# Hybrid decoder step: six pairs of gate tiles beside FoX in place of four, twelve single tiles beside the scans in place of sixteen

## The chip, the core and the metric

The kernel runs on one core of one Trainium2 chip. The metric is the device time of one execution in microseconds (us); less is better. Three runs of the kernel before gave 1921.46, 1922.18 and 1924.54 us, so its median is 1922.18 us.

## The reference

One layer of a hybrid decoder is computed for 1024 prompt tokens and 32 sample tokens, 1056 columns in all, with a model width of 1024. The tokens are normed, multiplied by one wide input projection, and the result feeds three token mixers: GLA (a gated linear scan), FoX (softmax attention with a forget bias) and HGRN2 (another gated scan). Each mixer's output goes through a branch matrix, is scaled by a sigmoid gate of its own, and the three are added:

```python
z = xn @ w_in      # gq gk gv glr gr | fq fk fv ff | hq hf hi hg | ga gb gc
merged = (sigmoid(ga) * (o_a @ w_branch_a) + sigmoid(gb) * (o_b @ w_branch_b)
          + sigmoid(gc) * (o_c @ w_branch_c))
x = x + merged @ w_out
x = x + (silu(h @ w_ffn_gate) * (h @ w_ffn_up)) @ w_ffn_down
```

What matters here are the 24 tiles of gates: ga, gb and gc have 1024 output rows each, which is 8 tiles of 128 rows each. A gate tile is nothing but a piece of the input projection; it is written to DRAM and read back when its branch tile is made.

## The kernel before

**Two ways to project a tile.** Every weight and activation is held as a high part and a low part, and a product is three TensorE matmuls (high by high, high by low, low by high). A single tile (`gemm`, L118) takes 3 column chunks of 352, 8 blocks of the inner dimension and 3 products: 72 matmuls of 352 columns, and three evictions by VectorE (L672, a multiply by the norm factor). A pair of tiles (`pair_run`, L1905) is made by a Strassen-like scheme with 7 products in place of 8: 7 products, 2 column quarters, 4 blocks, 3 products, that is 168 matmuls of 264 columns (L1941) for two tiles. Its weight sums, splits and evictions are VectorE and ScalarE work.

**Which tile goes which way.** `PAIRS` (L55 to L60) lists the tiles that go in pairs: 8 FoX tiles, 16 tiles for the scans, the gates GATES[24 - 2 * NGP:20] (at NGP = 4 these are gc 0 to 3), 12 tiles of gr, hq and hg, and gates gc 4 to 7. That is 44 tiles in 22 pairs. `TILES` (L61) are the rest: four FoX tiles, made early, and ga 0 to 7 and gb 0 to 7, made one by one.

**The stages around the change.**

1. `in_pairs` (L574) runs the 22 pairs. After each of a pair's 14 column quarters `beside` pumps one step of the FoX background work (`fox_head`, `fox_sample`), so a pair offers 14 steps. What is left at the end is drained (L637).
2. `phase_m` (L350) sets up the scans: two GLA pairs and four HGRN heads. They are generators in four queues: `bg3` and `bg4` (gates, decay, scan), `bgs` (the sample part of a scan) and `bgn` (`head_norm`, L1121). `bgn` runs one norm at a time, in order.
3. `mixer_jobs` (L676) projects the 16 single gate tiles. After each block of three matmuls `tick` (L195) pumps one step of one queue, in turn; when only one queue holds work, every second tick is skipped. So a tile offers 24 steps. The last tile is made by `gemm_tiles` (L151) and offers none.
4. `out_jobs` (L1577) makes 24 branch tiles, of 36 matmuls of 352 columns each, which offer 12 ticks each. The first eight are branch b (FoX), which doesn't need the scans. Before the last mixer tile, `first` (L1640) loads a gate and then asks for four free buffers for the FoX outputs; where they aren't free, it pumps steps with no matmuls between them:

```python
            while len(self.u.free) < 4:
                self.tick()
            ts.extend(fetch_o(order[0][0]))
```

5. After the sixth branch tile (AHEAD = 6, L1674) `ranges` (L1658) drains all four queues and then calls `any_range` (L1559), which reads a flag and branches (L1563): a recomputation of all scans that is skipped here. No instruction is laid across this branch, so all background work stands before it.

**A head norm** (`head_norm`, L1121) is: square on ScalarE (L1128), three matmuls of 352 columns with the ones matrix (L1135), three VectorE scalings (L1136), Ln and Exp on ScalarE (L1139, L1143), three VectorE steps of a Newton iteration (L1147, L1149, L1152), two VectorE multiplies (L1154, L1156), and a store (L1159).

**Order.** The program is laid out when the kernel is built: for each engine the instructions are put in an order in which those emitted earlier rank ahead of those emitted later, and one that isn't ready by the layout's own reckoning can be overtaken by a later one that is. On the chip each engine then keeps its order.

**After it** come the other 18 branch tiles, the output projection, the FFN in pairs, and the final norm. None of these is touched.

Of the kernel before, what the change touches and what calls it, by code (L numbers as in the profile page):

```python
# [50 lines left out]

FOX = [(n, h) for h in range(4) for n in ("fq", "fk", "fv")]
NFP = 4
NGP = 4
PAIRS = FOX[4:4 + 2 * NFP]  # L55
GATES = [(n, t) for n in ("ga", "gb", "gc") for t in range(8)]
PAIRS += [(n, t) for n, c in (("gq", 2), ("gk", 2), ("gv", 4), ("hf", 4), ("hi", 4)) for t in range(c)]
PAIRS += GATES[24 - 2 * NGP:20]
PAIRS += [(n, t) for n in ("gr", "hq", "hg") for t in range(4)]
# [2311 lines left out]
```

## Time and profile before

| what | us |
|---|---|
| median of three runs | 1922.18 |
| the profiled execution, its own time | 1923.73 |
| the profiled execution, span of the core | 1921.9 |
| last matmul of the pairs, first matmul of the single gate tiles | 651.08 |
| 11 of the 16 gate tiles done | about 871.6 |
| last matmul ahead of the branch at L1563 | about 1009.2 |
| first matmul behind it | 1015.05 |

The profiled execution's time is the span and 1.83 us around it, and it lies 1.55 us above the median. The page gives busy time of each engine over the span; the window view gives it for stretches, with the clock that was granted to TensorE as a share of full speed; the timeline gives instructions in the order of time, with the idle time of the engine before them and what released it.

### The profile page before, as it was taken

The numbers are of one execution on the slowest core, as the hardware profiler recorded it, in microseconds if no ns is written. First come the engines' busy times: TensorE is split into PE (matmuls) and PEld (weight loads), VectorE is DVE, ScalarE is ACT, GpSimd is POOL, SyncE is SP. The second block draws the span as 40 slices with busy tenths as digits, with TensorE's granted clock in tenths as the row PEclk, the third lists the DMA queues.
The fourth block names the chain that finished last, engine by engine and source line by source line (L and its number), as shares of the span: only waits on it lengthen the run. The fifth ranks groups of instructions, "written<-read, shape, count | busy, mean of one in ns | idle before, by whom it ended". The sixth has DMA issues, their size and how long they took to land. (4 is left out here: it accounts for less than half of the span.)

```text
span 1921.9 us, 36877 instructions
## 1 busy us (share of the span) xinstructions
PE 1894.2 (99%) x14846; PEld 1805.1 (94%) x14846; DVE 1322.9 (69%) x2395; ACT 836.9 (44%) x1470; POOL 44.0 (2%) x82
## 2 busy tenths in 40 slices
PE   9999999999999999999998999999999999999997
PEld 7999999999999988888898999999999999999997
DVE  7866656644666587687676755976666666568976
ACT  8444444322433355454554433634344333332435
POOL 0000000100000000000000000000000000000000
PEclk9999999999999999999998999999999999999999
DMA  4443332577666533343446443243331221423212
GB/s 170 163 146 116 115 127 83 170 238 243 205 210 186 186 115 138 125 147 131 140 159 235 147 146 116 86 153 127 120 104 68 78 99 55 182 93 117 87 61 91
DMA packets 99574, 263.33 MB, mean 137 GB/s; under 512 B 14850, under 2 KB 28354, under 8 KB 99394
## 3 DMA queue, kind: packets, MB, share of 16 engines
q1 hardware_dynamic: 97842, 259.69, 39.6%
q8 instruction: 118, 1.93, 0.4%
q10 hardware_dynamic: 1296, 0.67, 0.1%
q0 software_dynamic: 256, 0.52, 0.1%
q14 instruction: 62, 0.51, 0.1%
HBM read 188.60 MB, written 72.24 MB: 136 GB/s over the span
## 5 line engine op out<-in xcount | busy, mean ns | idle before, releaser
L139 PE MATMUL pg<-x,wh 128*128 128x352 f32 x1692 | 428.7, 334 | 6.7 <-DVE u L1622 6.0
L1941 PE MATMUL pg<-x,wh 128*128 128x264 f32 x2080 | 399.1, 287 | 0.9 <-DVE du L1950 0.5
L1941 PEld LDWEIGHTS pg<-x,wh 128*128 128x128 f32 x2080 | 322.8, 188 | 6.2 <-issue 2.6
L139 PEld LDWEIGHTS pg<-x,wh 128*128 128x128 f32 x1692 | 294.4, 189 | 28.3 <-issue 14.4
L1941 PE MATMUL pg<-x,wl 128*128 128x264 f32 x1040 | 295.5, 284 | 1.1 <-DVE wl L228 1.1
L139 PE MATMUL pg<-x,wl 128*128 128x352 f32 x846 | 275.1, 325 | 0.0
L1941 PEld LDWEIGHTS pg<-x,wl 128*128 128x128 f32 x1040 | 195.6, 188 | 1.6 <-DVE wl L228 1.6
L1941 PE MATMUL pg<-x,rh 128*128 128x264 f32 x976 | 186.2, 286 | 0.2 <-DVE fu L1950 0.2
L1941 PE MATMUL pg<-pr,wh 128*128 128x264 f32 x832 | 161.1, 291 | 0.0
L139 PEld LDWEIGHTS pg<-x,wl 128*128 128x128 f32 x846 | 160.4, 190 | 0.4 <-issue 0.3
L1941 PEld LDWEIGHTS pg<-x,rh 128*128 128x128 f32 x976 | 151.2, 188 | 2.0 <-issue 1.3
L227 ACT ACTIVATE wh<-wf 128x512 fp32r<-128x512 f32 (+2 forms) x125 | 77.5, 620 | 149.1 <-PE pg L1941 122.9
L1941 PE MATMUL pg<-x,rl 128*128 128x264 f32 x488 | 139.0, 285 | 0.0
L1941 PEld LDWEIGHTS pg<-pr,wh 128*128 128x128 f32 x832 | 129.0, 188 | 4.1 <-issue 2.6
L228 DVE TENSOR_TENSOR wl<-wf,wh 128x512 fp32r<-128x512 f32 (+2 forms) x125 | 84.9, 680 | 48.7 <-ACT wh L227 45.4
L1941 PE MATMUL pg<-pr,wl 128*128 128x264 f32 x416 | 118.3, 284 | 0.0
L110 ACT ACTIVATE wh<-wf 128x1024 fp32r<-128x1024 f32 (+2 forms) x60 | 51.4, 856 | 148.6 <-PE pg L139 125.3
L1950 DVE TENSOR_TENSOR pu<-pu,pg 128x264 f32<-128x264 f32 x132 | 56.1, 427 | 69.5 <-PE pg L1941 67.1
L1950 DVE TENSOR_TENSOR fu<-fu,pg 128x264 f32<-128x264 f32 x132 | 56.3, 429 | 66.7 <-PE pg L1941 66.5
L1952 ACT ACTIVATE fu<-pg 128x264 f32<-128x264 f32 x176 | 66.8, 384 | 62.7 <-PE pg L1941 62.7
L1952 ACT ACTIVATE pu<-pg 128x264 f32<-128x264 f32 x176 | 66.7, 382 | 62.6 <-PE pg L1941 62.2
L1941 PEld LDWEIGHTS pg<-x,rl 128*128 128x128 f32 x488 | 91.7, 188 | 0.1
(496 smaller groups left out, 3966.6 us busy)
## 6 DMA issues: line engine op xcount, KB each, us to landing
z_dram<-pu SPq DMA_DIRECT2D x44, 528.0 KB
wf<-in_wgu SPq DMA_DIRECT2D x44, 512.0 KB
u<-z_dram SPq DMA_DIRECT2D x38, 528.0 KB
wf<-in_winp SPq DMA_DIRECT2D x30, 512.0 KB
fa<-in_kc SPq DMA_DIRECT2D x48, 256.0 KB
fa<-in_vc SPq DMA_DIRECT2D x48, 256.0 KB
wf<-in_win SPq DMA_DIRECT2D x19, 512.0 KB
a_dram<-fu SPq DMA_DIRECT2D x18, 528.0 KB
```

Source lines behind the costliest of these rows:

```text
L110: nc.scalar.activation(wh[:, :n], wf[:, :n], AF.Copy)
L139: nc.tensor.matmul(ps[:m, :CW], a[:, k, :], b[:, sl], start=n == 0, stop=n == 3 * job.kt - 1)
L227: nc.scalar.activation(h, x, AF.Copy)
L228: nc.vector.tensor_tensor(l, x, h.bitcast(F32), ALU.subtract)
L1941: nc.tensor.matmul(ps, a[:, w], b, start=first and m == 0, stop=m == 3 * K - 1, skip_group_check=not first)
L1950: nc.vector.tensor_tensor(out, out, ps, ALU.add)
L1952: nc.scalar.activation(out, ps, AF.Copy)
```

## The change

One constant goes from 4 to 6. GATES[24 - 2 * NGP:20] grows from 4 tiles to 8, so gb 4 to 7 join the pairs (24 pairs in place of 22), placed just ahead of gc 0 to 3; `TILES` loses them, and 12 single gate tiles are left, with gb 3 the last of them in place of gb 7. AHEAD, the queues, the number of buffers and the order of the branch tiles stay.

```diff
 FOX = [(n, h) for h in range(4) for n in ("fq", "fk", "fv")]
 NFP = 4
-NGP = 4
+NGP = 6
 PAIRS = FOX[4:4 + 2 * NFP]
 GATES = [(n, t) for n in ("ga", "gb", "gc") for t in range(8)]
 PAIRS += [(n, t) for n, c in (("gq", 2), ("gk", 2), ("gv", 4), ("hf", 4), ("hi", 4)) for t in range(c)]
```

## Rows read from the trace of the kernel before

**Rows 1.** The page: span, and busy time of each engine.
```profile
span 1921.9 us, 36877 instructions
PE 1894.2 (99%) x14846; PEld 1805.1 (94%) x14846; DVE 1322.9 (69%) x2395; ACT 836.9 (44%) x1470; POOL 44.0 (2%) x82
```

**Rows 2.** Windows: stretch, length, busy of PE, PEld, DVE, ACT, POOL; granted clock; DMA.
```profile
676.00:871.60 195.60, 193.83 (x1417) 166.21 (x1415) 148.15 (x331) 103.03 (x170) 9.42 (x18) 1.00 0.35 123
871.60:895.70 24.10, 24.10 (x154) 20.80 (x155) 22.39 (x56) 13.00 (x28) 0.48 (x2) 1.00 0.36 125
871.60:1009.20 137.60, 136.75 (x871) 123.39 (x871) 98.56 (x183) 68.85 (x92) 0.48 (x2) 1.00 0.44 150
1009.20:1014.50 5.30, 0.00 (x0) 0.00 (x0) 0.72 (x2) 0.38 (x1) 0.00 (x0) 0.67 0.45 161
1015.00:1021.30 6.30, 6.25 (x21) 6.25 (x22) 1.38 (x3) 3.01 (x3) 0.00 (x0) 0.50 0.93 335
```

**Rows 3.** Windows, L139 alone (352 columns), then L1941 alone (264 columns).
```profile
1032.00:1196.00 164.00, 164.00 (x1015) 163.83 (x1014) 1.00 0.42 148
1232.00:1640.00 408.00, 408.00 (x3354) 408.00 (x3354) 1.00 0.28 99
```

**Rows 4.** Timeline of PE: last matmuls of FoX, first matmuls of the single gate tiles.
```profile
619.99 0.60 PE L1076 MATMUL pg<-f_ident,fa 128*128 128x128 f32 x4
...
651.08 0.49 PE L139 MATMUL pg<-x,wh 128*128 128x352 f32 x2
```

**Rows 5.** Timeline of DVE: eviction and weight split of a single tile.
```profile
871.06 0.53 DVE L672 TENSOR_TENSOR ub<-pg,r 128x352 f32<-128x352 f32 x1 [0.18 <-PE pg L139]
...
872.95 1.22 DVE L111 TENSOR_TENSOR wl<-wf,wh 128x1024 fp32r<-128x1024 f32 x1
```

**Rows 6.** Timelines of SP, DVE, PE: three instructions that show what is laid ahead.
```profile
889.56 0.33 SPq L1608 DMA_DIRECT2D u<-z_dram  x1
...
879.99 0.14 DVE L1548 TENSOR_REDUCE rg_m<-range 128x1 f32<-128x6 f32 x1
...
905.66 0.27 PE L1551 MATMUL pg<-c_ident,rg_m 128*1 128x128 f32 x1
```

**Rows 7.** Timeline of PE: matmuls of a head norm between those of a branch tile.
```profile
976.73 0.76 PE L1135 MATMUL pg<-ub,ones 128*128 128x352 f32 x2
977.06 0.76 PE L139 MATMUL pg<-x,wh 128*128 128x352 f32 x2
```

**Rows 8.** Timeline of DVE: the last head norm.
```profile
996.54 0.52 DVE L1136 TENSOR_SCALAR u<-pg 128x352 f32<-128x352 f32 x1
...
1001.13 1.26 DVE L1147 SCALAR_TENSOR_TENSOR u<-u,u 128x1056 f32<-128x1056 f32 x1 [0.60 <-ACT u L1143]
...
1002.74 1.25 DVE L1149 TENSOR_TENSOR u<-u,u 128x1056 f32<-128x1056 f32 x1
...
1004.34 1.25 DVE L1152 SCALAR_TENSOR_TENSOR u<-u,u 128x1056 f32<-128x1056 f32 x1
...
1006.10 1.31 DVE L1154 SCALAR_TENSOR_TENSOR ub<-ub,c_hng,u 128x1056 f32<-128x1056 f32 x1
1007.45 1.26 DVE L1156 TENSOR_TENSOR ub<-ub,u 128x1056 f32<-128x1056 f32 x1
```

**Rows 9.** Timeline of ACT: the same head norm, with a table load inside it.
```profile
997.09 1.09 ACT L1139 ACTIVATE u<-u 128x1056 f32<-128x1056 f32 x1 [4.66 <-DVE u L1136]
...
998.71 1.28 ACT L1143 ACT_TABLE_LOAD   x1
1000.01 1.09 ACT L1143 ACTIVATE u<-u 128x1056 f32<-128x1056 f32 x1
```

**Rows 10.** Timeline of SP: the store of the last head norm.
```profile
1008.74 0.33 SPq L1159 DMA_DIRECT2D o_dram<-ub  x1
```

**Rows 11.** Timeline of PE: either side of the branch at L1563.
```profile
1008.75 0.32 PE L139 MATMUL pg<-x,wl 128*128 128x352 f32 x1
1015.05 0.95 PE L139 MATMUL pg<-x,wh 128*128 128x352 f32 x2 [5.97 <-DVE u L1622]
```

## The prediction

> **What bounds the kernel now.** I began with the page: TensorE is busy for 1894.2 of 1921.9 us [rows 1], so a change pays by the TensorE time it removes, unless it uncovers something. Busy alone can hide waits, since matmuls are pipelined, so next I took the pace of gap-free stretches from the windows view: 164.00 us for 1015 matmuls of 352 columns is 0.1616 us each, 408.00 us for 3354 of 264 columns is 0.1216 us each [rows 3]. Then I read the stage that the change shortens, the scans. From 676 to 1009.2 us TensorE is never idle for long, and VectorE is busy for three quarters of the time [rows 2]. TensorE sets the time here, and the single tiles' matmuls are what covers the scans' waits. The timelines last: the last norm of the background work stores its result at 1008.74 us [rows 10], in the same microsecond in which the last matmul ahead of the branch starts [rows 11]. So background work and matmuls run out together at this point. That balance is what the change moves.
>
> **The matmuls.** Four single tiles go: 4 x 72 x 0.1616 = 46.5 us. Two pairs come: 2 x 168 x 0.1216 = 40.9 us. TensorE saves 5.7 us, if each stage stays covered. The added pairs need no FoX work beside them and give it no help: its last matmuls lie at 620 us, 31 us (one and a half pairs) ahead of the first single gate tile [rows 4], so the steps offered there find empty queues already. Weights and stores are as many bytes as before, only earlier on SP's queue. The gate tile gb 0 is stored three tiles ahead of its reload in place of seven, still over 30 us. The pairs' sums, splits and evictions stay under their matmuls, as in the FFN stretch, where TensorE is full [rows 3]. All this I cost at nothing.
>
> By a rule of the Trainium skill this part would come out otherwise. The page "TensorE: Matmul & The Clock Gate", section "Back-to-back issue gap", gives 81 ns per matmul at 128 columns and 131 ns at 512 for streams with weight loads; a straight line between them, an estimate, has 98.7 ns at 264 columns and 110.2 ns at 352, so two pairs would cost 33.2 us against 31.7 us for four tiles, and the sum below would end 7.1 us higher. The trace disagrees, with 121.6 and 161.6 ns, a ratio of 0.753 against 264/352 = 0.75 [rows 3]; I keep the measured pace.
>
> **What the four tiles covered.** The first eleven single tiles keep their place, so up to the point that was 871.6 us the scans go as before. Following the generators in the code from there, 136 background steps are left: five head norms (hgrn and GLA), the last HGRN head's gate and scan, and the sample scans. Before, four tiles took 96 of them, the six branch tiles 38, the drain 2. After, the twelfth tile is the last one and offers none. Its preparation asks for four free buffers; with the buffers held at that point it has to pump 28 steps before it gets them. The six branch tiles then offer 72, all used, since two queues or more hold work until the end. So 36 steps fall to the drain. In the order of the code these are the rest of one norm from its Newton steps on, and two whole norms.
>
> On paper the stretch 871.6 to 1009.2 us still fits: TensorE had 136.75 us [rows 2], of which 46.5 go, leaving 90.2. VectorE had 98.56 us; four tiles' evictions and splits (3 x 0.53 + 1.22 each [rows 5]) take off 11.2, leaving 87.4. Two nearly equal sums can only overlap fully if the order allows it, and the order doesn't: the drain's norms come after the sixth branch tile's matmuls, and behind them stands the branch, across which nothing can be laid.
>
> Could they be laid ahead of their turn? Loads and VectorE work are: a gate load emitted with the last tile, which begins at 951, is issued at 889.56, and the range reduction runs at 879.99, while its transpose on TensorE waits till 905.66 although its input has been there for 25 us [rows 6]. TensorE always has a ready matmul that was emitted earlier. Norm matmuls too sit at their own place between those of a branch tile [rows 7]. So a norm can start on ScalarE early, but gets past its ones-matmuls only when TensorE comes to them.
>
> **The tail, T.** After the sixth branch tile's last matmul there remain three times five VectorE steps (1.26 + 1.25 + 1.25 + 1.31 + 1.26 = 6.33 us a norm), six scalings of 0.52 us [rows 8], and Ln, Exp and a table load (1.09 + 1.28 + 1.09 us [rows 9]) that partly hide under VectorE. Upper bound: 3 x 6.33 + 6 x 0.52 + 3.5 = 25.6 us. Lower bound with this order: the first norm's steps and all scalings under the branch tile, 2 x 6.33 = 12.7 us. No reason fixes where between these it falls, so I take the middle, 19 us. If the layout did pull the norms' matmuls ahead, T would fall towards nothing; that is the first rival.
>
> Two corrections. Six norm matmuls move into the tail, where T already counts their wait: a ones-matmul starts 0.32 us after the one before [rows 7], so 6 x 0.32 = 1.9 us go. And the 28 forced steps stand ahead of the last tile with nothing of TensorE emitted between them: in 871.6 to 895.7 us, where 24 steps ran, VectorE was busy for 22.39 of 24.10 us [rows 2], so 28 keep it for some 26 us, and the background's own matmuls there (24.10 - 72 x 0.1616 = 12.5 us for 24 steps, 14.6 for 28) with the last tile's 11.6 make 26.2. Even; but the first branch tile waits for splits behind this work. A stall of 0 to 10 us is possible; I take 1, since the rows show TensorE full at that density.
>
> The branch itself costs 6 us of idle now and then 6.3 us at the granted clock of 0.50, which is 1.2 GHz, the lower of the two levels [rows 2, 11]. Both remain. With a longer idle ahead of it the slow stretch may last longer: 0 to 3 us (another 6.3 us at half pace), taken at 0.
>
> **Sum:** -5.7 + 19 - 1.9 + 1 = +12.4 us against the profiled execution's 1923.73 us. The same difference on the median, 1.55 us lower, gives 1934.6 us.
>
> **The rivals.** A measurement of this kernel can tell about 0.2% (3.8 us) from no change, so "same" is 1918.3 to 1926.0.
>
> *The norms are covered after all.* The layout finds gaps on TensorE in the denser stretch and pulls their matmuls forward, so that VectorE is done when TensorE is. For it: ScalarE and VectorE work is laid far ahead already [rows 6], and the two engines' sums are equal. Against it: the same rows on TensorE. Time: 1922.18 - 5.7 + 1 = 1917.5 us. It decides where T falls under 6.6 us, the point at which 5.7 + 1.9 - 1 is paid; under 2.8 us the gain can be measured. Chance 0.11.
>
> *Half covered:* T of 7 to 10 us, because gaps bring the first norm and part of the second forward: 1923 to 1926. Chance 0.11.
>
> *The forced steps stall TensorE as well,* 8 to 10 us in place of 1, with T at 19 to 22: 1942 to 1947. For it: VectorE at 93% in that density. Against it: TensorE full in the same row. Chance 0.13.
>
> *The pairing itself doesn't pay,* a pair beside the gates being held by its weight loads, so that two cost what four tiles cost: 1922.18 + 12.4 + 5.7 = 1940.3, against the pace of rows 3. Chance 0.02. *Nothing moves,* because gates leave one stage and their time appears whole in the other with everything covered: 1922. Chance 0.03.
>
> The forecast, T of 10 to 25.6 us and small stalls, 1926 to 1941: 0.60.
>
> **Range and chances.** 1919 to 1945 leaves out most of the first rival and the end of the third. Faster: the first rival, 0.11. Same: half covered and nothing moves, 0.14. Slower: the rest, 0.75.
>
> **What would show it.** Right: the first single gate tile some 41 us later; eleven tiles in the same 220 us; behind the sixth branch tile a stretch without matmuls of 18 to 30 us in place of 6, in which VectorE runs L1147 to L1156 three times and TensorE six L1135; half clock behind it; from there on everything shifted by a constant. Wrong: norm matmuls spread between branch matmuls and the idle stretch at 6 us again, or a gap ahead of the first branch tile of more than 3 us.

## The result and the profile after

Six pairs took 1939.27 us (median of 4 runs, 1936.63 to 1940.76) against 1921.82 us for four pairs in the same comparison (4 runs, 1921.33 to 1924.54). The ratio is 1.0085, with a 95% interval of 1.0073 to 1.0098. The kernel is slower, by 17.5 us on the medians. The two profiled executions differ by less, 1936.63 against 1923.73 us, or 12.9 us by their spans. What may have made part of the rest is told under "What was not expected".

The page of the kernel after, lines that answer to [rows 1]:

```profile
span 1934.8 us, 37040 instructions
PE 1887.2 (98%) x14894; PEld 1798.4 (93%) x14894; DVE 1334.9 (69%) x2417; ACT 856.6 (44%) x1503; POOL 49.0 (3%) x82
```

TensorE is busy for 7.0 us less than before, and the span is 12.9 us longer. The saving is there, and some 20 us of waiting came with it. The windows of the kernel after (the columns of [rows 2]) say in which stage:

```profile
690.00:871.60 181.60, 179.86 (x1306) 156.04 (x1306) 131.88 (x318) 93.42 (x160) 11.62 (x22) 1.00 0.41 143
871.60:996.00 124.40, 120.40 (x813) 103.77 (x812) 95.67 (x196) 83.51 (x112) 6.90 (x4) 1.00 0.43 147
996.00:1007.20 11.20, 9.80 (x50) 7.95 (x48) 9.03 (x12) 8.83 (x9) 0.00 (x0) 1.00 0.36 121
1007.20:1028.10 20.90, 0.01 (x1) 0.00 (x0) 14.49 (x16) 5.24 (x5) 0.00 (x0) 0.62 0.42 145
1028.10:1032.40 4.30, 4.28 (x15) 4.28 (x16) 0.83 (x2) 0.97 (x1) 0.00 (x0) 0.50 0.84 294
```

From 690 to 996 us TensorE loses 5.7 us in small waits. Then the sixth branch tile is done, and from 1007.2 us it has nothing for 20.9 us, in which VectorE works for 14.5. The timeline of TensorE in the kernel after names the waits; its first row answers to [rows 4], its last to [rows 11]:

```profile
690.07 0.48 PE L139 MATMUL pg<-x,wh 128*128 128x352 f32 x2
...
717.65 0.66 PE L1231 MATMUL pg<-c_ident,h 128*128 128x128 f32 x4 [1.08 <-ACT ub L761]
...
913.80 0.33 PE L1511 MATMUL pg<-c_ident,sti 128*128 128x128 f32 x1 [1.49 <-ACT sti L1507]
...
922.91 1.16 PE L1298 MATMUL pg<-u,h 128*128 128x128 f32 x8 [1.62 <-ACT h L1232]
...
996.00 1.94 PE L1135 MATMUL pg<-ub,ones 128*128 128x352 f32 x6
...
1000.14 2.04 PE L1135 MATMUL pg<-ub,ones 128*128 128x352 f32 x6 [1.40 <-ACT ub L1128]
...
1028.12 0.95 PE L139 MATMUL pg<-x,wh 128*128 128x352 f32 x2 [20.91 <-DVE u L1622]
```

The ones-matmuls of two whole norms stand behind the sixth branch tile, at 996.00 and 1000.14 us, where before they lay between a tile's matmuls [rows 7]. The idle ahead of the first matmul behind the branch is 20.91 us in place of 5.97 [rows 11]. VectorE's timeline in the kernel after, behind the sixth tile (compare [rows 8]):

```profile
996.20 0.53 DVE L1622 TENSOR_TENSOR u<-pg,ub 128x352 f32<-128x352 f32 x1
...
1008.49 1.25 DVE L1156 TENSOR_TENSOR ub<-ub,ub 128x1056 f32<-128x1056 f32 x1
...
1012.49 0.52 DVE L1136 TENSOR_SCALAR ub<-pg 128x352 f32<-128x352 f32 x1
1012.92 1.25 DVE L1156 TENSOR_TENSOR ub<-ub,ub 128x1056 f32<-128x1056 f32 x1
...
1017.34 1.26 DVE L1147 SCALAR_TENSOR_TENSOR ub<-ub,u 128x1056 f32<-128x1056 f32 x1 [2.56 <-ACT u L1143]
...
1022.58 1.26 DVE L1156 TENSOR_TENSOR u<-u,ub 128x1056 f32<-128x1056 f32 x1
1027.54 1.39 DVE L1622 TENSOR_TENSOR u<-pg,ub 128x352 f32<-128x352 f32 x3 [3.71 <-SPq L1563]
```

L1156 is the last step of a norm, and it stands here three times: three norms end behind the sixth tile. The last row is the key to the rest. These three evictions belong to the seventh branch tile. Its 36 matmuls (997.51 to 1007.2 us, with six ones-matmuls and a wait between them) ran ahead of the branch, but their evictions are emitted behind the drain, and VectorE comes to them only when the norms are done and the branch is passed. ScalarE in the last norm of the kernel after (compare [rows 9]):

```profile
1012.54 1.28 ACT L1139 ACT_TABLE_LOAD   x1 [4.83 <-DMA o_dram<-ub]
1013.83 1.08 ACT L1139 ACTIVATE ub<-ub 128x1056 f32<-128x1056 f32 x1
1014.93 1.28 ACT L1143 ACT_TABLE_LOAD   x1
1016.23 1.08 ACT L1143 ACTIVATE u<-ub 128x1056 f32<-128x1056 f32 x1
```

Its Ln writes into the buffer from which the first drained norm had just been stored, and waits for that store. Ln and Exp each pay a table load of 1.28 us.

### The profile page after: what moved, and what is told of

It is laid out like the page before. It is cut to its first block, busy times and chain, and to the rows that moved or that the text cites. A ratio compares the mean times of both kernels' runs of the same rounds, so it can differ in the third digit from the quotient of the medians.

```text
span 1934.8 us, 37040 instructions
## 1 busy us (share of the span) xinstructions
PE 1887.2 (98%) x14894; PEld 1798.4 (93%) x14894; DVE 1334.9 (69%) x2417; ACT 856.6 (44%) x1503; POOL 49.0 (3%) x82
## 5 line engine op out<-in xcount | busy, mean ns | idle before, releaser
L1941 PE MATMUL pg<-x,wh 128*128 128x264 f32 x2160 | 414.0, 287 | 0.9 <-DVE du L1950 0.5
L139 PE MATMUL pg<-x,wh 128*128 128x352 f32 x1500 | 378.5, 333 | 21.2 <-DVE u L1622 20.9
L1941 PEld LDWEIGHTS pg<-x,wh 128*128 128x128 f32 x2160 | 335.2, 188 | 6.1 <-issue 2.6
L1941 PE MATMUL pg<-x,wl 128*128 128x264 f32 x1080 | 306.7, 284 | 1.1 <-DVE wl L228 1.1
L139 PEld LDWEIGHTS pg<-x,wh 128*128 128x128 f32 x1500 | 260.5, 189 | 39.2 <-DVE u L1622 21.2
L139 PE MATMUL pg<-x,wl 128*128 128x352 f32 x750 | 244.1, 326 | 0.0
L1941 PEld LDWEIGHTS pg<-x,wl 128*128 128x128 f32 x1080 | 203.1, 188 | 1.6 <-DVE wl L228 1.5
L1941 PE MATMUL pg<-x,rh 128*128 128x264 f32 x1024 | 195.1, 286 | 0.3 <-DVE fu L1950 0.3
L1941 PE MATMUL pg<-pr,wh 128*128 128x264 f32 x928 | 178.9, 290 | 0.0
L1941 PEld LDWEIGHTS pg<-x,rh 128*128 128x128 f32 x1024 | 158.7, 188 | 2.0 <-issue 1.3
L1941 PEld LDWEIGHTS pg<-pr,wh 128*128 128x128 f32 x928 | 143.9, 188 | 4.1 <-issue 2.6
L227 ACT ACTIVATE wh<-wf 128x512 fp32r<-128x512 f32 (+1 forms) x129 | 80.0, 620 | 152.2 <-PE pg L1941 125.3
L1941 PE MATMUL pg<-x,rl 128*128 128x264 f32 x512 | 145.8, 285 | 0.0
L139 PEld LDWEIGHTS pg<-x,wl 128*128 128x128 f32 x750 | 142.0, 189 | 0.5 <-issue 0.3
L1941 PE MATMUL pg<-pr,wl 128*128 128x264 f32 x464 | 132.0, 284 | 0.0
L228 DVE TENSOR_TENSOR wl<-wf,wh 128x512 fp32r<-128x512 f32 (+1 forms) x129 | 87.7, 681 | 53.7 <-ACT wh L227 49.5
L1941 PEld LDWEIGHTS pg<-x,rl 128*128 128x128 f32 x512 | 96.3, 188 | 0.1
```

Of the source, the lines that this page charges most:

```text
L139: nc.tensor.matmul(ps[:m, :CW], a[:, k, :], b[:, sl], start=n == 0, stop=n == 3 * job.kt - 1)
L227: nc.scalar.activation(h, x, AF.Copy)
L228: nc.vector.tensor_tensor(l, x, h.bitcast(F32), ALU.subtract)
L1941: nc.tensor.matmul(ps, a[:, w], b, start=first and m == 0, stop=m == 3 * K - 1, skip_group_check=not first)
```

## The experiments

Each run was timed in five rounds beside the kernel before. In kernels with added lines, line numbers are up to 5 higher than in the kernel after (L1625 and L1626 are then the eviction L1622, L1163 the store L1159, L140 the matmul L139).

**Is it the branch?** Two runs leave out the branch with the recomputation it guards.

```diff
-            self.any_range([t for t in merged if t is not None])
```

> Six pairs, with the branch at L1563 left out (the flag is still computed; the recomputation that it guards, and that these data never need, is not in the program). My theory: what costs time is that the last head norms stand ahead of a point across which no branch tile covers them. Without that point they lie under the branch tiles that follow, the idle stretch of 21 us goes, and the saving of the pairs shows: 5.7 us (5 to 7) less than the kernel with four pairs and no branch, so about 1906 to 1910 us. Rival A, the denser scans stall TensorE ahead of the drain: the difference stays above 0, by whatever the stall is. Rival B, a pair costs what two single tiles cost: the difference is 0 within 2 us.

> Four pairs, with the branch left out in the same way: the control for the run above. All theories: the 6 us of idle at the branch and about half of the 6.3 us at the lower clock behind it go, so 8 to 10 us less than before, about 1912 to 1914 us.

Six pairs took 1934.07 us, four pairs 1922.23; ratios to before 1.006 (1.0047 to 1.0074) and 0.9996 (0.9987 to 1.0005). Both expectations fell. Taking the branch out is worth 5 us with six pairs and nothing clear with four, and six pairs are still 11.8 us above four. In the kernel with six pairs and no branch, the timeline of VectorE, then that of TensorE, then the window of the wait (columns as in [rows 2]):

```profile
1013.13 1.25 DVE L1156 TENSOR_TENSOR ub<-ub,ub 128x1056 f32<-128x1056 f32 x1
1014.29 1.38 DVE L1622 TENSOR_TENSOR u<-pg,ub 128x352 f32<-128x352 f32 x3
```
```profile
1014.87 0.95 PE L139 MATMUL pg<-x,wh 128*128 128x352 f32 x2 [7.96 <-DVE u L1622]
```
```profile
1006.90:1014.87 7.97, 0.01 (x2) 0.00 (x1) 7.97 (x10) 3.38 (x4) 0.00 (x0) 0.78 0.73 220
```

VectorE is busy for all of the 7.97 us in which TensorE stands: it works through norms while the seventh tile's results wait to be evicted, so TensorE has no accumulator to go on in. The norms were emitted in one lump ahead of these evictions, and VectorE keeps that order. No branch is needed for that wait.

The kernel with four pairs and no branch waits at the same place, which is why leaving the branch out gave it nothing. Its row of TensorE, then two windows of it, then the same two with six pairs (columns as in [rows 2]):

```profile
1013.30 0.93 PE L139 MATMUL pg<-x,wh 128*128 128x352 f32 x2 [5.39 <-DVE u L1622]
```
```profile
1012.00:1035.00 23.00, 21.70 (x118) 21.73 (x119) 15.24 (x27) 9.86 (x11) 0.00 (x0) 0.85 0.66 225
1035.00:1100.00 65.00, 65.00 (x404) 65.00 (x403) 45.24 (x82) 22.56 (x26) 0.00 (x0) 1.00 0.41 129
```
```profile
1012.00:1035.00 23.00, 16.88 (x72) 15.54 (x72) 16.99 (x21) 14.84 (x15) 0.00 (x0) 0.72 0.91 306
1035.00:1100.00 65.00, 62.45 (x375) 62.12 (x376) 46.84 (x84) 23.06 (x27) 0.00 (x0) 0.97 0.45 150
```

So the wait itself is only 2.6 us longer with six pairs, and it begins 1.0 us earlier. The other 10.2 of the 11.8 us come behind it, up to the FFN's pairs (from 1014.87 to 1220.13 us in place of 1013.30 to 1208.32). With six pairs TensorE idles there for a further 5.8 us, and it spends more time at the lower clock. The idle time is waits of 1.00, 1.07 and 0.50 us for splits and an eviction, with VectorE busy throughout from 1020 to 1030 us, and one of 3.06 us at 1037.37 us for an eviction whose gate came late. Why that gate came late was not followed.

**Is it the order, and how does the loss grow?** The first of these two kernels pumps two steps per block in the six branch tiles; the second makes five pairs.

```diff
                 self.tick()
+                if job.more:
+                    self.tick()
...
+            job.more = n < AHEAD
```

> Six pairs; each block of three matmuls in the six branch tiles ahead of the branch pumps two steps in place of one, so that the drain finds empty queues. Same work, same buffers, other order. My theory, by which the order puts the norms late and not a lack of VectorE time: the idle stretch ahead of the branch falls from 21 us to 8 to 14, and the time to 1924 to 1931 us. Rival A, VectorE has no room for the work under the branch tiles: what leaves the drain comes back as stalls between the branch tiles' matmuls, and the time stays at 1935 to 1939. Rival C, the buffer that the last norm waits for and the table loads make the tail: the last norm still ends late, idle stays at 17 us or more, 1934 or more.

> NGP = 5: five pairs of gates and 14 single tiles, half of the change. By the order of the code the drain then holds two norms, one of them begun, in place of two whole ones and a part, and no step is forced ahead of the last gate tile. My theory: -2.9 us for one pair in place of two tiles, and an idle stretch of 11 to 13 us in place of 6 and 21, so +2 to +5 us against before, 1924 to 1927 us: the loss is not proportional. Rival A, stalls from forced steps: none here, so about -2 us against before if they were the loss. Rival B, pairs don't pay: 1927 to 1930.

The run with two steps took 1925.28 us (ratio 1.0008, 0.9999 to 1.0017), 14 us less than six pairs without it: the same work in another order. TensorE's first matmul behind the branch in it:

```profile
1015.91 0.95 PE L140 MATMUL pg<-x,wh 128*128 128x352 f32 x2 [7.59 <-DVE u L1625]
```

Five pairs took 1925.91 us (ratio 1.0014, 1.0005 to 1.0023), with this row of TensorE:

```profile
1019.11 0.95 PE L139 MATMUL pg<-x,wh 128*128 128x352 f32 x2 [12.81 <-DVE u L1622]
```

5.97, 12.81 and 20.91 us of idle for none, one and two pairs more. Both times fell inside what the order predicts, and 7.59 us of idle is just below the 8 to 14 expected. The order put the norms late; VectorE's time was there, but not early enough for all of it, as 7.59 us of idle are left.

**Do the pairs pay at all?** More steps are now pumped over the whole stage: every third block pumps two with six pairs, every eighth with four.

```diff
                 self.tick()
+                self.blocks += 1
+                if self.blocks % 3 == 0:
+                    self.tick()
```

> Six pairs, and every third block of three matmuls, in the twelve single tiles and the branch tiles, pumps two background steps in place of one; by the code some 48 offers are then left over before the drain, which finds empty queues. Same work, same branch. My theory as it now stands (the runs without the branch moved the time by 5 us only, so what costs is that the last norms come to VectorE in one lump and TensorE waits for evictions behind it): nothing is left to uncover, the 5.7 us of the pairs show, and the 6 us of idle at the branch shrink as well, so 1911 to 1917 us. Rival A, VectorE has no room for a denser stream (75 per cent busy now): more stalls of 1 to 2 us like the two in the scans, 1920 to 1930 us.

> Four pairs, with every eighth block pumping two steps, which leaves about as many offers over (55) as in the run above: its control. My theory: the idle at the branch shrinks from 6 us to 1 to 3, so 1917 to 1920 us, and the run above is 5 to 7 us below this one, the price of the pairs alone. Rival B, a pair costs what two single tiles cost: no difference within 2 us.

1916.44 us (ratio 0.9967, 0.9954 to 0.9979) and 1916.18 us (0.9962, 0.9950 to 0.9974). Both beat the kernel before, and they don't differ, where my theory had 5 to 7 us between them: rival B's number, but not for its reason. Three views of the kernel with six pairs (VectorE: the sixth tile's last eviction; SyncE: the last norm's store; TensorE: the first matmul behind the branch):

```profile
994.13 0.53 DVE L1626 TENSOR_TENSOR u<-pg,ub 128x352 f32<-128x352 f32 x1
```
```profile
998.97 0.33 SPq L1163 DMA_DIRECT2D o_dram<-u  x1
```
```profile
1006.06 0.96 PE L140 MATMUL pg<-x,wh 128*128 128x352 f32 x2 [6.14 <-DVE u L1626]
```

and the same three of the kernel with four pairs:

```profile
1000.03 0.53 DVE L1626 TENSOR_TENSOR u<-pg,ub 128x352 f32<-128x352 f32 x1 [1.42 <-PE pg L140]
```
```profile
986.56 0.32 SPq L1163 DMA_DIRECT2D o_dram<-u  x1
```
```profile
1001.38 0.40 PE L140 MATMUL pg<-x,wl 128*128 128x352 f32 x1 [1.06 <-PEq L1567]
```

With six pairs the sixth tile is done 5.9 us earlier: that is the saving of the pairs, 5.7 us, in full. (The single tiles begin at 690.20 us in place of 649.38, and from there to this eviction it is 303.9 us in place of 350.7.) But the last norm is stored 12.4 us later, and 5.1 us more of idle at the branch give the gain back. The count of offers in the expectation was wrong for six pairs: by the code, a queue that is alone skips every second one, so the last step was emitted in the sixth tile and nothing was left over.

**Is it the buffer, or the table loads?** The first edit gives a norm's working buffers back ahead of its output, the second asks for one set of tables ahead of the drain.

```diff
-        self.u.put(o, *slots)
+        self.u.put(*slots, o)
```
```diff
+            self.tab = None
             self.drain(self.bg3, self.bg4, self.bgs, self.bgn)
```

> Six pairs; a head norm gives its three working buffers back ahead of its output buffer, so that the last norm no longer writes into the buffer whose store it had to wait for. Same work and order otherwise. My theory, by which the work of three norms in a lump is the loss: the chain gets at most 3 us shorter, 1936 to 1939 us. Rival C, the wait for the store makes the tail: 6 us or more less, 1933 or below.

> Six pairs; ahead of the drain ScalarE is told to load the one set of tables that holds Ln and Exp, so that the drained norms need no load of 1.28 us before each. Four loads go from the tail and one comes, but only those of the last norm were waited for by VectorE: -2.6 us by my theory, 1936 to 1938 us. Rival C, ScalarE's chain is what the tail consists of: 4 us or more less, 1935 or below. If the loads lie under VectorE's work after all: no difference, 1938 to 1940.

1941.09 us (ratio 1.0094, 1.0081 to 1.0107) and 1940.27 us (1.0088, 1.0075 to 1.0101): no gain from either, and both a little above what was expected. With the other buffer the wait for the store is gone from ScalarE, and another has its place:

```profile
1017.00 1.08 ACT L1139 ACTIVATE ub<-ub 128x1056 f32<-128x1056 f32 x1 [4.03 <-DVE ub L1136]
```

Ln now waits for the last norm's scaling, which VectorE has in its order behind the steps of the two other norms. In the kernel after it stood there too, at 1012.49 us, just behind the store's end. Two waits end together, and taking one away moves little: the idle ahead of the branch is 18.95 us. That the time did not fall by these 2 us has another reason, told under "What was not expected". The second edit did not do what it was meant to. ScalarE in that run still loads a table ahead of each Ln and Exp, so the price of the loads stays open:

```profile
1015.02 1.28 ACT L1139 ACT_TABLE_LOAD   x1 [4.84 <-DMA o_dram<-ub]
1016.32 1.08 ACT L1139 ACTIVATE ub<-ub 128x1056 f32<-128x1056 f32 x1
1017.42 1.28 ACT L1143 ACT_TABLE_LOAD   x1
```

**Could the norms be done in time with six pairs?** As the two denser runs, and a lone queue skips nothing; then five pairs with every fourth block doubled.

```diff
-        self.pause = max(0, 2 - sum(map(bool, qs)))
+        self.pause = 0
```

> As the denser run with six pairs, and a queue that is alone no longer skips every second offer (in that run the skips used up what I had counted as left over: the last norm was emitted in the sixth branch tile, and on the chip it stored at 998.97 us, 12.4 us later than in its control, so TensorE idled 6.14 us at the branch in place of 1.06 although it had 36 matmuls more behind it). Now the last step is emitted three branch tiles earlier, as in the control. My theory, by which the pairs save 5.7 us wherever the norms are done in time: the idle falls to 1 to 2 us and the time to 1910 to 1913 us, 4 to 6 below the control. Rival A, VectorE itself has no room: the last norm still stores at 996 us or later, and the time stays at 1915 to 1918.

> As the denser run with four pairs, and a lone queue skips no offers: the control for the run above. Its norms were already done in time and its idle at the branch was 1.06 us, so no difference to that run by either theory: 1915 to 1918 us.

> Five pairs, every fourth block pumping two steps, and a lone queue skipping none, so that the last step is emitted one branch tile ahead of the first. My theory: half the price of two pairs and nothing uncovered, 2.9 us below the control with four pairs, 1912 to 1915 us. Rival A: 1915 or more.

Six pairs 1919.97 us (ratio 0.9981, 0.9971 to 0.9991), four 1923.70 (1.0003, 0.9994 to 1.0012), five 1915.58 (0.9958, 0.9945 to 0.9972). Six pairs are 3.7 us below their control. But both medians are above those with the skips, which neither theory expected: the control clearly, by 7.5 us; six pairs by 3.5 us, with intervals that just overlap and eleven runs from 1913.72 to 1922.96 us. The profiled execution with six pairs took 1916.87 us, 3.1 us below its median, so its trace can't show all of what slowed the others. TensorE in the kernel with six pairs:

```profile
983.28 0.96 PE L140 MATMUL pg<-x,wh 128*128 128x352 f32 x2 [2.98 <-DVE u L1626]
...
1004.20 0.40 PE L140 MATMUL pg<-x,wl 128*128 128x352 f32 x1 [1.72 <-PEq L1567]
```

The idle at the branch fell from 6.14 to 1.72 us, and 2.98 us of waiting for evictions came ahead of it: norms in quick succession hold up the branch tiles' evictions, as the lump of the drain does. Behind that wait TensorE ran at the lower clock (columns as in [rows 2]):

```profile
983.30:988.00 4.70, 4.70 (x16) 4.70 (x17) 2.18 (x5) 3.76 (x4) 0.00 (x0) 0.50 0.48 171
```

So the 4.4 us won at the branch were lost again ahead of it. The control shows the same; its window around a wait of 2.73 us at 962.53 us (columns as in [rows 2]) has VectorE busy throughout:

```profile
960.00:970.00 10.00, 7.47 (x46) 7.47 (x47) 10.00 (x12) 4.54 (x5) 0.00 (x0) 1.00 0.65 241
```

The last norm with six pairs was stored at 996.80 us, 2.2 us earlier than with the skips although its last step was emitted three tiles earlier: rival A's bound. The norms were not had much earlier there. Why the control lost all of 7.5 us is only partly seen: 2.73 us are this wait, and its profiled execution had also come to the single tiles 2.5 us later, ahead of anything that the edit touches.

**And without the branch?** The denser run with six pairs, the branch left out.

> The denser run with six pairs, with the branch left out as in the first run. There the branch was all that the late norms still met: 6.14 us of idle, against 1.06 in the control with four pairs, while TensorE had done 36 matmuls (5.8 us) more by the same time. My theory, pairs save 5.7 us of TensorE and only what stands behind the last norm takes it back: 5 to 7 us less than with the branch, 1909 to 1912 us, so below the control with four pairs at 1916. Rival A, VectorE's evictions stand behind the norms as well and hold TensorE without any branch: 1914 to 1917 us.

1907.18 us (ratio 0.9913, 0.9899 to 0.9926), even lower than expected. TensorE's longest wait between 985 and 1030 us in it:

```profile
1000.53 0.92 PE L140 MATMUL pg<-x,wh 128*128 128x352 f32 x4 [0.59 <-ACT wh L111]
```

9.3 us below the same kernel with the branch: 6.14 us are the idle, and the stretch at the lower clock behind it is gone (granted clock 1.00 from 1000 to 1010 us, in place of 0.59). Against the first run, also without a branch, it is 27 us less. So the lump and the branch are two ways to expose the same norms, each holds TensorE by itself, and of the kernels with six pairs only the one with both gone is clearly below 1916 us. That this is the pairs' 5.7 us kept is not shown, since its control, four pairs pumped denser and without the branch, was not run. With four pairs and the branch TensorE had 1.06 us of idle at the branch and 2.5 us of waits in the 16 us behind it, so part of the 9.3 us may be there with four pairs too. This version leaves out the fallback and is no replacement. Of the kernels that do all the work, five pairs with denser pumping was the lowest, but the three near 1916 us can't be told apart.

## Why the prediction was right, point by point

**The time.** 1934.6 us was forecast, 1939.27 measured, inside 1919 to 1945. Against its own profiled execution the sum said +12.4 us, and the spans differ by 12.9. That the two agree to half a microsecond is luck: the stall came out 4.6 us larger than forecast, the tail 2.2 us, the step from four tiles to two pairs 1.9 us and the stretch at the lower clock 0.6 us smaller, and these nearly cancel. On the medians the kernel lost 17.5 us, 5 us more than the sum.

**The matmuls** (-46.5 and +40.9). Right. The single tiles begin at 690.07 us, against 649.38 in the denser kernel with four pairs: 40.7 us for two pairs. (In the profiled execution before they began at 651.08, some 2 us late against other executions with four pairs, so the difference to it is 39.0.) The estimate from the Trainium skill, page "TensorE: Matmul & The Clock Gate", section "Back-to-back issue gap", had 33.2 us for the two pairs; these rows disagree with it, as those of the prediction did. The whole saving was seen in the denser kernels, as a lead of 5.9 us at the sixth tile. The first eleven single tiles took the same 220 us as before: the last of their evictions starts at 910.04 us, before at 871.06 [rows 5].

**A stall of 1 us.** Mis-sized, though its bounds of 0 to 10 held. From the first single tile to the last matmul ahead of the branch it was 358.0 us before and 317.1 after, 40.9 less in place of 46.5. Of the 5.6 us lost, 4.5 are waits: TensorE idles in this stretch for 7.1 us in place of 2.6. The forced steps have the largest, 1.49 and 1.62 us at 913.80 and 922.91; another 1.40 us are the wait at 1000.14 us, behind the sixth tile. I had looked at VectorE's 22.39 us of 24.10 [rows 2]; it was ScalarE that was full. The window of the kernel after:

```profile
906.00:924.00 18.00, 14.89 (x119) 11.26 (x116) 11.42 (x29) 17.82 (x25) 0.21 (x1) 1.00 0.35 116
```

ScalarE 17.82 of 18.00 us, VectorE 11.42. The rival of 8 to 10 us of stalls had the right place and too high a price. With denser pumping neither wait is there.

**The tail** (19 us, less 1.9). Near in size, 14.9 us more idle at the branch, but made otherwise. From the sixth tile's end at 996.0 us to VectorE's last step at 1023.84 it was 27.8 us, above the upper bound of 25.6, since the last norm waited for a store, for VectorE's order and for two table loads, and the bound held one table load alone. Of this 11.2 us lay under work that I had not counted: the seventh tile's 36 matmuls (997.51 to 998.74 and 1001.75 to 1007.2, 6.7 us), the ones-matmuls of two norms (1.5 and 1.6 us from their start to the next matmul, where the prediction took 1.9 us for both) and 1.4 us of waiting among them. 16.6 us were bare. "Behind them stands the branch, across which nothing can be laid" failed: TensorE went on across it until its accumulators were full. What can't cross is the evictions. The kernel before shows the same. VectorE there, the last eviction of the sixth tile and the three of the seventh:

```profile
1003.90 0.52 DVE L1622 TENSOR_TENSOR u<-pg,ub 128x352 f32<-128x352 f32 x1
...
1014.47 1.39 DVE L1622 TENSOR_TENSOR u<-pg,u 128x352 f32<-128x352 f32 x3 [4.16 <-DVEq L1563]
```

So the last matmul ahead of the branch, at 1008.75 us [rows 11], was the seventh tile's too, and the last norm's steps up to 1008.71 us [rows 8] lay under that tile. Background work and matmuls did run out together, but with seven tiles of cover and not six.

**Why it was exposed.** The prediction named the branch. The runs without it show that this was only part of the mechanism: of the 17 us between six and four pairs, 11.8 are there without any branch. There VectorE's own order holds the evictions behind the norms, and the waits and the lower clock that follow make most of the difference.

**Norm matmuls not pulled forward.** Right, 996.00 and 1000.14 us. **The clock,** 0: right in the profiled execution, where the stretch at 0.50 is 4.3 us in place of 6.3 [rows 2]. From there to the first long run of the FFN's pairs it took 0.6 us less than before. Sum of the stages: +39.0 - 40.9 + 14.9 - 0.6 = +12.4 us.

## What to carry to other kernels

Work that an engine takes out of a stage was also cover for the stage's other work: count what is left to be covered in emitted steps, not in sums of busy time. VectorE kept the emitted order here and met the lump of norms ahead of the evictions that TensorE needed. When an optimisation loses, first spread the background work to the new length of the stage; here that took 6.8 us off the kernel with four pairs, more than the 5.7 us that the change could have saved, and some 23 us off the one with six. Then look which engine fills up next: with six pairs the last norms were hardly had earlier, and the gain and its price met at the same time of 1916 us.

## What was not expected

A short stall amid dense work cost more than its length. With the other buffer, TensorE waited 2.86 us in the forced steps, and the granted clock fell to the lower level, 1.2 GHz. The same followed the wait of 2.98 us in the kernel with six pairs and no skips. TensorE's row and the windows of that run (columns: stretch, length, PE busy, granted clock, DMA):

```profile
915.23 2.08 PE L1298 MATMUL pg<-ub,h 128*128 128x128 f32 x8 [2.86 <-ACT h L1232]
```
```profile
905.00:915.20 10.20, 7.37 (x69) 0.98 0.08 27
915.00:920.00 5.00, 4.77 (x15) 0.50 0.83 271
920.00:925.00 5.00, 5.00 (x36) 0.83 0.18 69
```

In the profiled execution of the kernel after, with waits of 1.49 and 1.62 us at this place, it stayed at 1.00. Two of its other three executions had spans of 1938.9 and 1939.0 us at a mean granted clock of 0.990 against 0.993; they may have met this stretch, but there is no trace of them. Executions also differ by 2 to 3 us in the first 650 us, which the change doesn't touch: with four pairs the single tiles began at 649.08 to 651.89 us. A difference of 2 us between the totals of two single profiles of this kernel says nothing.
